# Scan masks merged ahead of one exponential, other PSUM banks for the first rows of the output projection, and another landing rule in the planner

## The chip, the cores and the metric

The kernel runs on one core of a Trainium2 chip. A core has five engines that work side by side, each through its own queue in order: TensorE (PE, with its weight loads PEld), VectorE (DVE), ScalarE (ACT), GpSimd (POOL) and SyncE (SP, which issues most transfers here). The metric is the device time of one execution in microseconds (us), lower being better; three executions of the kernel before took 971.27, 972.96 and 973.4 us, with the median 972.96.

## What is computed

One layer of a diffusion backbone over 512 latent tokens (width 1024) with a context of 256 tokens. Both are normalised, modulated and multiplied with one combined input matrix, and the result feeds two groups of heads: attention (16 heads; latent queries see latent and context keys) and a state-space scan that runs forwards and backwards (16 heads in 2 groups, chunks of 128 tokens). Both go through one output projection; a gated MLP with a width-3 convolution follows. The part that the change rewrites is the sum inside a chunk of the scan:

```python
def segment_decay(cum):
    diff = cum[..., :, None] - cum[..., None, :]
    mask = jnp.tril(jnp.ones((n, n), dtype=bool))
    return jnp.exp(jnp.where(mask, diff, -jnp.inf))
...
within = segment_decay(a_cum)
cb = jnp.einsum("bclgn,bcsgn->bcgls", cc, bc)
y_diag = jnp.einsum("bcgls,bcgels,bcsgep->bclgep", cb, within, xd)
...
y_x = ssd_output(st_xf[0], st_xf[1]) + flip(ssd_output(st_xb[0], st_xb[1]))
...
y = y + d_skip.reshape(SSD_GROUPS, HEADS_PER_GROUP, 1) * xs
```

For one head and one chunk the forward scan needs a matrix that is zero above the diagonal, the backward scan one that is zero below it. Both are multiplied by the same `cb` and by the same inputs, so that they can be added first.

## The kernel before, in words

All matrix products are split into a high and a low float32r part and summed as three products (lines 503, 757, 1184, 1314, 1546), so that a block of work is: DMA, a copy on ACT (L502), a subtraction on DVE or POOL (L503), and products of 128x512 or 128x256 on PE.

The program runs through these stages: the modulation and the gate of the scan (L689); the input projections with their convolutions (`xbc`, L757 to L803); the scan (`ssd`, once for each group of 8 heads) beside the attention (`pair_of_heads`, 8 pairs of heads, with `project` ahead of each); the output projection (`natural_gemm`, L1314); the MLP's up-projection (L757 again) and its down-projection (`sweep`, L1546).

**The masks.** In `ssd`, for two chunks at a time (`cp2`) and each of 8 heads (`e`), so 2 x 2 x 8 = 32 times in all, one step builds the mask of both directions for two chunks. PE spreads the running sums over the partitions with two products of 128x256 (L1031, `sel`) into one PSUM bank, then adds a table that holds 0 or -1e30 with one product of 128x512 (L1035, `capi` and `caps`). ACT takes four exponentials of 128x128 with a bias for each row (L1040: direction by chunk). POOL adds the two directions (L1044), and DVE multiplies the sum by `cbt`, the products of B and C (L1045). L1064 multiplies the result with the inputs. L1050 starts the chunk's output with the skip term, `xs` times `dsk`. The tables `capf` and `capb` come with the constants, and POOL copies them once (L772, L774).

**PSUM.** There are 8 banks of 512 columns. `bk.cut` hands them out by name. While the scan runs, all of its products share one bank, number 7 (`s`). Attention has banks 0 to 2 for scores (`sc`), 3 for its sums (`o`), 4 and 5 for transposes (`t`) and 6 for projections (`p`). When the scan is done, bank 7 joins `t`. The output projection then takes four pairs of banks for its four blocks of 128 rows, block 0 in banks 0 and 1, and so on to block 3 in banks 6 and 7.

**The order.** Nothing above is the order in which the engines run it. The program is first recorded, then `plan` sets the order of every engine's queue. It prices each instruction (`price`), runs a list schedule forwards and backwards (`Graph.schedule`), places the buffers (`Memory`), and repeats; the order it finds is imposed on the program. For a transfer it keeps the time at which the queue of transfers is free again, and expects the data when that transfer's own cost is over, with `DMA_WAIT` (910) and 0.8 of the cost (`DMA_ALONE`) on top, in `Graph.wait`.

## Time and profile before

| | |
|---|---|
| median of three executions | 972.96 us |
| the profiled execution's own time | 974.93 us |
| its span, first to last instruction | 973.1 us |
| what lies around the span | 1.83 us |
| PE, PEld, DVE, ACT, POOL busy, share of the span | 98%, 83%, 77%, 55%, 25% |
| the 32 mask steps begin and end | 193.0 and 402.0 us |
| granted TensorE clock, mean | 0.990 |

A busy PE is not a PE at its peak: products overlap in its pipeline, and a product's recorded time is longer than the distance to the next one. Idle time of an engine costs something only where another engine waits for it. In the lists of groups, a row gives the line, the engine, the operation, output<-input, the shape and the count, then the busy time in us, the mean of one in ns, and the idle time ahead of them with what ended it.

### The profile page before, as it was taken

What the parts mean: (1) busy time and instruction counts of PE and PEld (TensorE: products, weight loads), DVE (VectorE), ACT (ScalarE), POOL (GpSimd) and SP (SyncE); (2) the same over time, 40 slices, a digit from 0 to 9 for tenths busy, and PEclk for the clock granted to TensorE, in tenths of its full rate; (3) what the DMA queues carried; (4) which work ended last, traced back from release to release, by engine and by line L of the source; (5) the groups of instructions that cost most, each with busy time, mean ns of one, the idle gap of its engine ahead of it and who ended that gap; (6) DMA issues with size and microseconds to landing.
All of it is one profiled execution on the core that took longest, in us unless ns stands there. A gap on an engine that the chain in (4) does not pass through costs nothing.

```text
span 973.1 us, 14739 instructions
## 1 busy us (share of the span) xinstructions
PE 949.4 (98%) x5150; PEld 809.9 (83%) x5150; DVE 749.7 (77%) x1377; ACT 538.8 (55%) x1088; POOL 240.0 (25%) x249
## 2 busy tenths in 40 slices
PE   9999999999999999999999999999999999999995
PEld 8888898888788888888888887988888888887784
DVE  5898868888879887887899977945275332899898
ACT  4464337655777887789877215634223221447673
POOL 0001000846758455643000000000010150330021
PEclk7999999999999999999999999999999999999998
DMA  9933102011323432544668666233273212545783
GB/s 354 377 116 141 40 15 78 21 49 50 96 60 83 95 104 66 130 104 115 214 199 302 216 223 231 67 152 130 78 262 115 66 66 91 170 143 194 232 280 135
DMA packets 54586, 137.66 MB, mean 141 GB/s; under 512 B 8032, under 2 KB 10992, under 8 KB 54512
## 3 DMA queue, kind: packets, MB, share of 16 engines
q1 hardware_dynamic: 53712, 135.05, 42.9%
q10 hardware_dynamic: 800, 1.68, 0.5%
q8 instruction: 40, 0.66, 0.3%
q14 instruction: 34, 0.28, 0.1%
HBM read 114.63 MB, written 6.34 MB: 124 GB/s over the span
## 4 chain that ended last, share of the span: by engine, by line
PE 75%; DVE 14%; DMA 5%; ACT 3%; issue 3%; SPq 0%; POOL 0%; DVEq 0%; ACTq 0%; POOLq 0%
PE banks L757 40%; PE banks L1314 8%; DVE block L503 7%; PE banks L689 5%; PE banks L1184 4%; PE banks L1546 4%; DMA block<-block 2%; PE banks L1200 2%; DMA block<-in_wdn_dram 2%; PE banks L1212 2%; DVE smalls L1186 2%; DVE block L1539 1%; PE banks L1119 1%; PE banks L1016 1%; PE banks L601 1%
## 5 line engine op out<-in xcount | busy, mean ns | idle before, releaser
L757 PE MATMUL banks<-block,block 128*128 128x512 f32 (+1 forms) x2132 | 443.8, 361 | 2.4 <-DVE block L1410 2.0
L757 PEld LDWEIGHTS banks<-block,block 128*128 128x128 f32 x2132 | 357.2, 189 | 62.8 <-DVE block L1410 2.2
L503 DVE TENSOR_TENSOR block<-block,block 128x512 fp32r<-128x512 f32 (+4 forms) x316 | 248.5, 824 | 78.9 <-PE banks L757 34.3
L502 ACT ACTIVATE block<-block 128x512 fp32r<-128x512 f32 (+5 forms) x340 | 217.1, 665 | 139.9 <-PE banks L757 33.6
L1546 PE MATMUL banks<-block,block 128*128 128x512 f32 x462 | 108.7, 392 | 1.9 <-DVE block L503 1.6
L1546 PEld LDWEIGHTS banks<-block,block 128*128 128x128 f32 x462 | 86.0, 188 | 22.9 <-DVE block L503 4.5
L1184 PE MATMUL banks<-block,block 128*128 128x256 f32 (+1 forms) x384 | 97.2, 354 | 2.3 <-DMA block<-block 1.1
L503 DVE TENSOR_TENSOR block<-banks,block 128x256 fp32r<-128x256 f32 (+1 forms) x156 | 83.4, 556 | 12.4 <-ACT block L502 11.4
L1314 PE MATMUL banks<-block,block 128*128 128x512 f32 x384 | 89.2, 391 | 0.0
L1314 PEld LDWEIGHTS banks<-block,block 128*128 128x128 f32 x384 | 71.8, 188 | 14.5
L502 ACT ACTIVATE block<-banks 128x256 fp32r<-128x256 f32 (+1 forms) x156 | 74.1, 497 | 10.7 <-PE banks L1200 7.5
L1186 DVE TENSOR_REDUCE smalls<-banks 128x1 f32<-128x768 f32 x64 | 60.9, 952 | 18.3 <-PE banks L1184 12.7
L1188 ACT ACTIVATE block<-banks,smalls 128x768 f32<-128x768 f32 x64 | 57.9, 904 | 20.5 <-DVE smalls L1186 18.2
L1184 PEld LDWEIGHTS banks<-block,block 128*128 128x128 f32 x384 | 60.8, 189 | 9.7 <-ACT block L1188 2.6
L1200 PE MATMUL banks<-cst,block 128*128 128x128 f32 x384 | 66.4, 274 | 2.2 <-DVE block L503 2.1
L1212 PE MATMUL banks<-block,block 128*128 128x256 f32 x384 | 68.0, 294 | 0.2
L792 DVE SCALAR_TENSOR_TENSOR block<-banks,cwh,block 128x510 f32<-128x510 f32 (+3 forms) x88 | 51.5, 621 | 15.9 <-ACT block L788 15.1
L591 DVE SCALAR_TENSOR_TENSOR block<-block,block 128x1024 f32<-128x1024 f32 x52 | 62.4, 1216 | 0.5 <-PE banks L757 0.4
L1212 PEld LDWEIGHTS banks<-block,block 128*128 128x128 f32 x384 | 56.0, 190 | 4.4 <-DVE block L1245 0.5
L1441 ACT ACTIVATE block<-banks,prm 128x512 f32<-128x512 f32 x22 | 17.1, 777 | 73.2 <-PE banks L757 73.1
L1200 PEld LDWEIGHTS banks<-cst,block 128*128 128x128 f32 x384 | 47.5, 141 | 10.7 <-DVE block L503 4.2
L1040 ACT ACTIVATE block<-banks,block 128x128 f32<-128x128 f32 x128 | 42.1, 372 | 15.4 <-PE banks L1035 13.1
(230 smaller groups left out, 1104.3 us busy)
## 6 DMA issues: line engine op xcount, KB each, us to landing
block<-in_wdn_dram SPq DMA_DIRECT2D x99, 256.0 KB
block<-in_wmod_dram SPq DMA_DIRECT2D x48, 512.0 KB
block<-in_wup_dram SPq DMA_DIRECT2D x44, 512.0 KB
block<-block SPq DMA_DIRECT2D x32, 256.0 KB
block<-in_wout_dram SPq DMA_DIRECT2D x16, 512.0 KB
block<-in_wxbc_dram SPq DMA_DIRECT2D x12, 512.0 KB
block<-block SPq DMA_DIRECT2D x40, 128.0 KB
block<-in_wz_dram SPq DMA_DIRECT2D x16, 256.0 KB
```

The costliest lines, as they stand in the source:

```text
L502: act(hi, src, AF.Copy)
L503: (lo_eng or V).tensor_tensor(out=lo, in0=src, in1=hi, op=ALU.subtract)
L591: V.scalar_tensor_tensor(out=junk, in0=wt, scalar=0.5, in1=vec, op0=ALU.mult, op1=ALU.mult, accum_out=acc)
L757: mm(po, lhsT=wf(k, pt[0]), rhs=xf(k, pt[1]), start=(k == 0 and pt == parts[0]), stop=(k == nk - 1 and pt == parts[-1]))
L792: V.scalar_tensor_tensor(out=st[:, lo:hi], in0=pm[:, lo + d : hi + d], scalar=cwh[:, m * 5 + j : m * 5 + j + 1], in1=st[:, lo:hi], op0=ALU ...
L1184: mm(sc[:, o : o + n], lhsT=q_[:, x_, qi * P : (qi + 1) * P], rhs=kk[:, y_, :], start=part == 0, stop=part == 2)
L1186: V.reduce_max(nm, sc[:, :T], axis=AX.X, negate=True)
L1188: act(pe, sc[:, :T], AF.Exp, bias=nm, scale=1.0, accum_out=sum_)
L1200: nc.tensor.transpose((tx if c < NX else tc_)[:, o : o + P], pe[:, s_ : s_ + P], ident)
L1212: mm(po[:, half * 256 : half * 256 + 256], lhsT=vst(c), rhs=rhs, start=(part == 0 and c == 0), stop=(part == 1 and c == NKT - 1))
L1314: mm(po[i][:, nh * 512 : nh * 512 + 512], lhsT=l[lp][:, i * P : (i + 1) * P], rhs=w[wp][:, nh * 512 : nh * 512 + 512], start=(k == 0 and l ...
L1546: mm(po[i], lhsT=l[:, lp, i * P : (i + 1) * P], rhs=w[wp], start=first and q == 0 and n == 0, stop=q == PAIRS[-1] and n == 2, skip_group_c ...
```

## The change

Three edits are made together.

1. The masks. The product with the table and the tables themselves go. Of a mask, one triangle now comes from the forward direction and the other from the backward one, in one matrix. DVE adds to the forward half of the bank the difference of the two biases (`nbd`, two instructions of 128x128 that read PSUM), then copies the backward half over it wherever the table `trib` is not zero (`copy_predicated`, 128x256). ACT takes two exponentials of 128x128 instead of four, from SBUF instead of PSUM, and POOL multiplies by `cbt` straight away, so that DVE's product L1045 goes. On the diagonal both directions count, and only one is left there; what is missing, `dt` times the diagonal of `cbt`, moves into the skip term: for each group POOL cuts out the diagonal (one product of 128x512), DVE sums it (one `reduce_sum`) and makes `skip` with four small instructions.
2. The banks. The four pairs for the output projection are dealt in the reverse order, so that block 0 has banks 6 and 7, and bank 7 is taken out of `t` before the last pair of heads.
3. The planner. A transfer in a full queue is expected earlier: at the later of its own start plus 1.8 of its cost and the time the queue is free less `DMA_FULL` (600); `DMA_WAIT` stays. For a transfer that finds the queue empty the sum is as before. `price` gets a rule for `copy_predicated`.

```diff
-DMA_START, DMA_WAIT, DMA_AHEAD, DMA_ALONE, RUN, FLYING = 650, 910, 3000, 0.8, 80, 8
+DMA_START, DMA_WAIT, DMA_AHEAD, DMA_ALONE, RUN, FLYING, DMA_FULL = 650, 910, 3000, 0.8, 80, 8, 600
...
-        return DMA_WAIT + DMA_ALONE * self.cost[i] if self.dma[i] else WAITS.get((self.eng[i], self.eng[j]), 0)
+        return DMA_WAIT if self.dma[i] else WAITS.get((self.eng[i], self.eng[j]), 0)
...
-                end[i] = queue = max(t + self.dma[i] + DMA_START, queue) + self.cost[i]
+                began = t + self.dma[i] + DMA_START
+                queue = max(began, queue) + self.cost[i]
+                end[i] = max(began + (1 + DMA_ALONE) * self.cost[i], queue - DMA_FULL)
...
+    V.tensor_tensor(out=nbd, in0=nb[:, :NX, :16], in1=nb[:, :NX, 16:], op=ALU.subtract)
...
+        G.tensor_tensor(out=dg.rearrange("p (c n) -> p c n", c=NX), in0=cbt.rearrange("p (c n) -> p c n", c=NX),
+                        in1=ident.unsqueeze(1).to_broadcast([P, NX, P]), op=ALU.mult)
+        V.reduce_sum(cbd[:, g * NX : g * NX + NX], dg.rearrange("p (c n) -> p c n", c=NX), axis=AX.X)
+        for c in range(NX):
+            V.scalar_tensor_tensor(out=skip[:, c, g * 8 : g * 8 + 8], in0=dtb_[:, c, g * 8 : g * 8 + 8],
+                                   scalar=cbd[:, g * NX + c : g * NX + c + 1], in1=dsk[:, g * 8 : g * 8 + 8], op0=ALU.mult,
+                                   op1=ALU.add)
...
-                       rhs=chl[:, cp2 * 256 : cp2 * 256 + 256], start=dir_ == 0, stop=False)
-
-                mm(pdf, lhsT=capi, rhs=caps, start=False, stop=True)
-                df = t2()
-                for dir_ in range(2):
-                    for j in range(2):
-                        o = (dir_ * 2 + j) * P
-                        act(df[:, o : o + P], pdf[:, o : o + P], AF.Exp,
-                            bias=nb[:, cp2 * 2 + j, dir_ * 16 + h : dir_ * 16 + h + 1])
+                       rhs=chl[:, cp2 * 256 : cp2 * 256 + 256], start=True, stop=True)
+
+                df, at = t2(P, 2, P), slice(cp2 * 256, cp2 * 256 + 256)
+                for j in range(2):
+                    V.tensor_scalar(out=df[:, j, :], in0=pdf[:, j * P : (j + 1) * P], scalar1=nbd[:, cp2 * 2 + j, h : h + 1],
+                                    scalar2=None, op0=ALU.add)
+                V.copy_predicated(df, sooner, pdf[:, 256:].rearrange("p (c n) -> p c n", c=2))
                 pfree(pdf)
-                Me = M[e // 4][:, e % 4, :]
-                G.tensor_tensor(out=Me, in0=df[:, :256], in1=df[:, 256:], op=ALU.add)
-                V.tensor_tensor(out=Me, in0=Me, in1=cbt[:, cp2 * 256 : cp2 * 256 + 256], op=ALU.mult)
+                for j in range(2):
+                    act(df[:, j, :], df[:, j, :], AF.Exp, bias=nb[:, cp2 * 2 + j, 16 + h : 17 + h])
+                G.tensor_tensor(out=M[e // 4][:, e % 4, :], in0=df.rearrange("p c n -> p (c n)"), in1=cbt[:, at], op=ALU.mult)
...
+            if hp == NPAIR - 1:
+                bk.free["t"].remove(bank(7))
...
-    bk.cut(sc=[], o=[], t=[], p=[], a=[two(0), two(2), two(4), two(6)])
+    bk.cut(sc=[], o=[], t=[], p=[], a=[two(6), two(4), two(2), two(0)])
```

The planner's new prices move instructions nearly everywhere. Two places matter below. The first is DVE's queue in the third group of masks, where the second group of heads is scanned beside the attention. Before, in the kernel's own lines (L1186 is the softmax's maximum, L503 a low part, L1045 the mask's product):

```order
L503 TENSOR_TENSOR block_118_684<-banks,block_118_684 128x2x128
L503 TENSOR_TENSOR block_154_888<-banks,block_154_888 128x256
L1045 TENSOR_TENSOR block_498_3044<-block_498_3044,block_16_130 128x256
L1186 TENSOR_REDUCE smalls<-banks 128x1
L503 TENSOR_TENSOR block_374_2450<-banks,block_334_2263 128x4x128
L503 TENSOR_TENSOR block_118_684<-banks,block_118_684 128x2x128
L1045 TENSOR_TENSOR block_498_3044<-block_498_3044,block_16_130 128x256
L1186 TENSOR_REDUCE smalls<-banks 128x1
```

And after, where a line stands some lines lower or higher in the file (L1194 is the maximum, L504 a low part, L1047 the added bias, L1049 the copy under the table):

```order
L504 TENSOR_TENSOR block_343_2286<-banks,block_343_2286 128x2x128
L1047 TENSOR_SCALAR block_84_510<-banks,block_106_614 128x128 x2
L1194 TENSOR_REDUCE smalls<-banks 128x1
L1049 COPY_PREDICATED block_84_510<-block_74_468,banks 128x256
L504 TENSOR_TENSOR block_31_273<-banks,block_31_273 128x256
L504 TENSOR_TENSOR block_418_2644<-banks,block_116_681 128x4x128
L1047 TENSOR_SCALAR block_84_510<-banks,block_106_614 128x128 x2
L504 TENSOR_TENSOR block_118_683<-banks,block_118_683 128x2x128
L1049 COPY_PREDICATED block_84_510<-block_74_468,banks 128x256
```

Between two maxima stood one mask instruction, and it read SBUF alone; now three stand there, they read the scan's bank, and a maximum can lie between the first two and the third.

The second place is PE's queue where attention ends and the output projection begins. Before (L1212 is attention's last product, L1314 the output projection):

```order
L1212 MATMUL banks<-block_718_4483,block_160_948 128x256 x4
L1314 MATMUL banks<-block_284_1940,block_719_4484 128x512
L1314 MATMUL banks<-block_441_2799,block_719_4484 128x512
L1212 MATMUL banks<-block_486_2966,block_94_524 128x256 x2
L1212 MATMUL banks<-block_676_4200,block_160_948 128x256 x4
L1314 MATMUL banks<-block_284_1940,block_719_4484 128x512
L1212 MATMUL banks<-block_486_2966,block_94_524 128x256 x2
L1314 MATMUL banks<-block_284_1940,block_719_4484 128x512
```

And after (L1220 is attention's last product, L1324 the output projection, L1208 a transpose of the softmax):

```order
L1220 MATMUL banks<-block_657_4033,block_757_4687 128x256 x2
L1324 MATMUL banks<-block_797_5045,block_25_230 128x512 x2
L1208 MATMUL banks<-cst,block_788_4941 128x128 x2
L1324 MATMUL banks<-block_161_944,block_25_230 128x512
L1220 MATMUL banks<-block_632_3787,block_159_939 128x256 x4
L1324 MATMUL banks<-block_161_944,block_25_230 128x512
L1324 MATMUL banks<-block_797_5045,block_25_230 128x512
L1324 MATMUL banks<-block_161_944,block_25_230 128x512
L1220 MATMUL banks<-block_685_4220,block_757_4687 128x256 x2
```

Ahead of attention's last product, 21 products of the output projection stand in the queue before, and 24 after. In the output projection's own run PE's order is the same as before for some 400 products.

More of the change, by code (lines that the diff above doesn't have):

```diff
@@ L33 @@
 GRID_W = 64
-BIG = 1e30
 PRM = {}
@@ L65, in constants @@
     put("trib", (i[:, None] >= i[None, :]))
-    put("capf", np.where(i[:, None] <= i[None, :], 0.0, -BIG))
-    put("capb", np.where(i[:, None] >= i[None, :], 0.0, -BIG))
     rot = np.zeros((64, P))
```

30 lines of the change are left out of this document (16 added, 14 removed).

## The prediction

> **What bounds the kernel now.** I read the page first: the span, each engine's busy time, and the chain that ended last.
>
> ```profile
> span 973.1 us, 14739 instructions
> PE 949.4 (98%) x5150; PEld 809.9 (83%) x5150; DVE 749.7 (77%) x1377; ACT 538.8 (55%) x1088; POOL 240.0 (25%) x249
> PE 75%; DVE 14%; DMA 5%; ACT 3%; issue 3%; SPq 0%; POOL 0%; DVEq 0%; ACTq 0%; POOLq 0%
> ```
>
> PE is busy for 98% of the span, and three quarters of the chain are PE's own work. The last quarter is what PE waited for, above all DVE (14%). These shares serve below as weights: a microsecond taken from PE is worth at least 0.75 us, one put on DVE costs 0.14 us on average, one taken from ACT brings 0.03 us.
>
> Then the stages, by windows. The first row is the stretch from the first mask step to the last, the second what follows up to the output projection, the third a stretch of the up-projection in which PE waits for nothing, the fourth the fullest stretch of DVE that I found among the masks.
>
> ```profile
> 193.00:402.00 209.00, 206.20 (x1268) 178.13 (x1267) 176.86 (x298) 156.14 (x390) 124.76 (x121) 1.00 0.30 76
> 402.00:514.00 112.00, 108.75 (x751) 97.15 (x751) 93.16 (x167) 91.38 (x196) 31.71 (x37) 1.00 0.57 162
> 802.00:826.00 24.00, 24.00 (x108) 19.88 (x106) 6.56 (x11) 3.27 (x7) 0.69 (x1) 1.00 0.28 88
> 292.00:316.00 24.00, 23.59 (x143) 19.94 (x142) 23.11 (x33) 18.45 (x41) 21.05 (x20) 1.00 0.32 83
> ```
>
> The columns are the length, then busy time of PE, PEld, DVE, ACT and POOL, the granted clock, and the DMA share. While the masks are made PE is busy for 206.2 of 209 us, DVE for 176.9 (85%), ACT for 156.1 (75%). So PE leads there, and DVE is the next engine, with 32 us to spare.
>
> **The change part by part.** The masks' rows, and the nearest rows for what is new:
>
> ```profile
> L1031 PE MATMUL banks<-block,sel 128*128 128x256 f32 x64 | 14.2, 291 | 0.4 <-DVE block L1066 0.3
> L1035 PE MATMUL banks<-block,capi 128*128 128x512 f32 x32 | 12.7, 396 | 0.0
> L1314 PE MATMUL banks<-block,block 128*128 128x512 f32 x384 | 89.2, 391 | 0.0
> L1040 ACT ACTIVATE block<-banks,block 128x128 f32<-128x128 f32 x128 | 42.1, 372 | 15.4 <-PE banks L1035 13.1 <-POOL block L1044 1.3 <-DVE block L503 0.7
> L1044 POOL TENSOR_TENSOR block<-block 128x256 f32<-128x256 f32 x32 | 29.8, 935 | 36.9 <-ACT block L1040 28.7 <-issue 5.4 <-PE banks L757 2.8
> L1045 DVE TENSOR_TENSOR block<-block,block 128x256 f32<-128x256 f32 x32 | 20.2, 652 | 2.1 <-POOL block L1044 2.0
> L503 DVE TENSOR_TENSOR block<-banks,block 128x256 fp32r<-128x256 f32 x74 | 30.3, 415 | 4.3 <-ACT block L502 3.8
> L503 DVE TENSOR_TENSOR block<-banks,block 128x512 fp32r<-128x512 f32 x82 | 55.5, 683 | 8.1 <-ACT block L502 7.6 <-PE banks L1200 0.2
> L1410 DVE SCALAR_TENSOR_TENSOR block<-banks,mod,block 128x128 fp32r<-128x128 f32 x32 | 10.0, 340 | 0.5 <-ACT block L1409 0.4
> L533 DVE SCALAR_TENSOR_TENSOR smalls<-smalls 128x1 f32<-128x1 f32 x48 | 7.4, 157 | 0.6
> ```
>
> *PE loses L1035.* One product lasts 396 ns in the record, but overlaps its neighbours. In a full queue one of 128x512 takes 24.00 us / 108 = 0.222 us by the window and 89.2 / 384 = 0.232 us by L1314. So 32 products are worth 7.1 to 7.4 us of queue; I take 7.3. The two products of L1031 stay. If PE were the chain throughout the masks, all 7.3 us would come off; by the weight of 0.75 it is 5.5. I take 5.5 and keep 7.3 for the range.
>
> *DVE gains.* L1045 goes, 20.2 us. For each of 32 steps come two added biases of 128x128 from PSUM. The nearest row is L1410, the same size from PSUM, with a second tensor: 0.340 us. Half of L503's 0.415 us for 256 columns, 0.208, is the lower bound. I take 0.27. The copy under the table reads 256 columns of PSUM and a table in SBUF, as L503 reads PSUM and SBUF: 0.415 us at least. It shows nowhere before; if it passed its two sources in turn it would be as long as L503 with 512 columns, 0.683. I take 0.45, near the row of its own size. The sum is 64 x 0.27 + 32 x 0.45 = 31.7 us (26.6 to 43.6). For each group a sum over 512 columns (as L503, 0.68) and four small instructions (as L533, 0.16) add 2 x 1.3 = 2.6 us. The net is 31.7 + 2.6 - 20.2 = +14 us, between +9 and +26. The 32 us that DVE has to spare beside PE hide most of it; by the weight of 0.14 it costs 2.0 us (1.3 to 3.6).
>
> The Trainium skill, "SBUF — State Buffer", says that a GpSimd instruction and a VectorE instruction with two SBUF inputs lock each other out of a shared pair of ports for a whole instruction. The trace agrees: L1045, with two SBUF inputs, means 652 ns, L503 of the same size with one input in PSUM 415. By that rule the new instructions, which read PSUM, are never held, DVE's net falls to the lower bound of +9 us, and its cost to 1.3.
>
> *ACT loses half its exponentials.* 128 of them take 42.1 us, 0.33 each. 64 stay, reading SBUF and no longer PSUM; from SBUF they are not shorter, and at most as long as the recorded 0.372. So ACT gives back 42.1 - 64 x 0.36 = 19 us, worth 0.03 x 19 = 0.6 us. POOL has 32 instructions of the same size in L1044's place, and three or four more at the start of the groups; it is no part of the chain (0%), and its 209 - 124.8 = 84 us of idle time among the masks hide them.
>
> *The scan's bank.* One step of the third group, in order of time:
>
> ```profile
> 323.33 0.50 PE L1031 MATMUL banks<-block,sel 128*128 128x256 f32 x2
> 323.67 0.40 PE L1035 MATMUL banks<-block,capi 128*128 128x512 f32 x1
> 324.16 1.14 ACT L1040 ACTIVATE block<-banks,block 128x128 f32<-128x128 f32 x4 [0.46 <-PE banks L1035]
> 325.43 0.74 POOL L1044 TENSOR_TENSOR block<-block 128x256 f32<-128x256 f32 x1 [3.16 <-ACT block L1040]
> ```
>
> Bank 7 is held from 323.33 until the exponentials end at 325.30, 2.0 us. After, PE needs 0.2 us less, and three DVE instructions (2 x 0.27 + 0.45 = 1.0 us) take the place of 1.14 us of ACT; where a maximum stands between them, as in the order above, the bank is held a maximum longer. I cost this at nothing, since PE has attention's products meanwhile; without that cover it is one maximum for a part of the 32 steps, and that is the first rival's matter.
>
> *The banks of the output projection.* PE's rows at the handover:
>
> ```profile
> 514.15 0.94 PE L1314 MATMUL banks<-block,block 128*128 128x512 f32 x3
> 515.29 1.86 PE L1314 MATMUL banks<-block,block 128*128 128x512 f32 x7
> 517.61 0.99 PE L1200 MATMUL banks<-cst,block 128*128 128x128 f32 x6 [0.45 <-DVE block L503]
> 522.40 0.86 PE L1314 MATMUL banks<-block,block 128*128 128x512 f32 x3
> ```
>
> The output projection already fills gaps here, since block 3 had bank 6 early. The new order brings 24 instead of 21 products ahead of attention's end: 3 x 0.23 = 0.7 us at most, if each fills a hole. Against it the last pair has two banks for transposes and no longer three, and PE's waits at transposes are the longest of its list:
>
> ```profile
> PE banks L1200 <- DVE block L503: 2.1, 5, 0.6
> PE banks L757 <- DVE block L1410: 2.0, 1, 2.0
> PE banks L1546 <- DVE block L503: 1.6, 3, 1.1
> ```
>
> Five waits make 2.1 us there; doubling them costs 2.1. So this part lies between -0.7 and +2.1 us; I take -0.2, near the first, since the order shows other products beside the transposes.
>
> *The planner.* Its landing rule matters only where the queue of transfers is full: the first 50 us, the output projection, the down-projection. In the first, SP's order is the same at the start; in the second, PE's is the same for 400 products. What can change is in waits like the last row, 1.6 us. The rest is that every queue in the middle is dealt anew. I take 0, with +-2 us.
>
> The sum: -5.5 + 2.0 - 0.6 - 0.2 + 0 = -4.3 us. The profiled execution took 974.93 us (span 973.1 and 1.83 around it), 1.97 above the median of 972.96; from it the sum gives 970.6, from the median 968.7. I forecast 968.5.
>
> **The rivals.** *DVE takes over from PE among the masks, and the kernel is slower.* It would have 176.9 + 14 = 190.9 us to do in a stretch that PE would leave in 209 - 7.3 = 201.7: 95% full. The fourth window shows that DVE can be so full (23.11 of 24), but only for 24 us. If it reaches 90% in the mean, the stretch takes 190.9 / 0.90 = 212 us, 3 longer than now; at the upper bound of +26 it takes 225, 16 longer. From 0.90 x 209 - 176.9 = 11.2 us of added work on, this decides. For it speaks that the new instructions stand between PE's product and the bank's release, among the softmax's maxima; against it that the planner can spread the masks over the 112 us behind (DVE 83%), and that ACT is eased. The price is +3 to +16; I put it at +4, 977 us. The Trainium skill, "Perfetto Trace Analysis", section "Optimizing Scalar/DVE Operations", says that work may move from DVE to Scalar where DVE is saturated, and that each DVE instruction on PSUM pays about 125 ns beside its elements. The change goes the other way, with 96 such instructions, 12 us by the page (an estimate); no run yet shows whether 85% counts as saturated.
>
> *Nothing comes of it.* PE's products gone, the chain runs through the softmax (score, maximum, exponential, transpose), which waits for DVE as before, and new waits of 7 us take the place of the work. Then the time is 973, within 2 us. For it speaks the quarter of the chain that is not PE's; against it the 98.7% of PE among the masks.
>
> *More than the sum.* If all 7.3 us come off, ACT's 13.1 us of waits for L1035 go with its in-order queue, and half of PE's listed 5.7 us of waits above close, the gain is 7.3 + 2.9 = 10 us: 963.
>
> **How the numbers follow.** This kernel's runs can tell about 0.2%, 2 us, from no change. I give the forecast (2 to 8 us faster) 0.52, more than that 0.18, nothing 0.15, DVE in the lead 0.15. Faster is then 0.70, same 0.15, slower 0.15. The range from 961 to 974.5 holds the forecast, nearly all of the case of no change, and the larger gain up to 12 us (its 10, and the planner's 2 on top); it leaves out most of the slower case and the end of the larger gain, some 0.2. The bounds of the unknown prices (-7.3 + 1.3 - 0.6 - 0.7 - 2 = -9.3; -5.5 + 3.6 - 0.6 + 2.1 + 2 = +1.6) give 963.7 to 974.6 and lie in it but for 0.1 us.
>
> **What would show it.** After the change the row of L1035 is gone and PE's busy time is about 7 us less; the exponentials are 64 with 21 to 24 us; the added biases come at 0.21 to 0.34 us and the copy at 0.42 to 0.68; DVE's busy time grows by 9 to 26 us, and PE's share of the stretch of masks stays at 98% or more. The sum is wrong if the stretch from the first mask to the output projection is not 4 to 8 us shorter, if PE's waits for DVE there grow by more than 3 us, or if the gain lies outside of it, at the handover or in the stages with a full queue.

## The result, and the profile after

The changed kernel takes 977.88 us (median of 20 runs, 972.12 to 983.47); the kernel before, beside it on the same chip, 972.83. The ratio is 1.0057 with a 95% interval from 1.0041 to 1.0072: the change makes the kernel 0.6% slower, 5.5 us. The prediction was 968.5, within 961 to 974.5.

The profiled execution of the kernel after is one of its quicker ones (976.18 us, span 974.4). First its page: the span, the busy time of each engine, the chain that ended last.

```profile
span 974.4 us, 14684 instructions
PE 946.4 (97%) x5118; PEld 805.6 (83%) x5118; DVE 768.6 (79%) x1452; ACT 525.2 (54%) x1024; POOL 244.3 (25%) x246
PE 75%; DVE 14%; DMA 4%; ACT 3%; issue 2%; SPq 0%; POOL 0%; DVEq 0%; ACTq 0%
```

PE has 32 instructions less and DVE is busy for 18.9 us more (768.6 against 749.7), yet the shares of the chain are those of before. They say nothing of what happened.

Next the groups of the mask step. L1041 are the two products that stayed, L1047 the added biases, L1049 the copy under the table, L1052 the exponentials, L1053 the product on POOL.

```profile
L1041 PE MATMUL banks<-block,sel 128*128 128x256 f32 x64 | 14.2, 298 | 3.0 <-DVE block L1049 2.4 <-DVE block L1031 0.6
L1047 DVE TENSOR_SCALAR block<-banks,block 128x128 f32<-128x128 f32 x64 | 21.1, 342 | 1.1 <-PE banks L1041 0.8
L1049 DVE COPY_PREDICATED block<-block,banks 128x256 f32<-128x256 int32 x32 | 14.2, 443 | 0.3
L1052 ACT ACTIVATE block<-block,block 128x128 f32<-128x128 f32 x64 | 22.6, 397 | 7.5 <-DVE block L1049 5.8 <-DVE smalls L533 1.6
L1053 POOL TENSOR_TENSOR block<-block,block 128x256 f32<-128x256 f32 x32 | 24.4, 767 | 35.4 <-ACT block L1052 25.8 <-PE banks L1192 4.0 <-DVE block L504 2.8
```

The products of L1041 waited 0.4 us in all before (L1031 then); now it is 3.0 us, 2.4 of it for L1049, the copy that ends the use of the bank.

Then two windows. Of the kernel before, the first 16 mask steps and all 64 products of the masks:

```profile
193.00:260.70 67.70, 67.39 (x399) 57.91 (x398) 57.34 (x95) 42.99 (x110) 41.68 (x36) 1.00 0.20 52
193.00:396.50 203.50, 200.70 (x1231) 173.02 (x1230) 171.75 (x289) 151.29 (x379) 122.20 (x117) 1.00 0.29 74
```

and of the kernel after, the same two stretches:

```profile
217.60:267.60 50.00, 46.60 (x283) 40.33 (x282) 46.98 (x105) 33.07 (x77) 34.35 (x34) 1.00 0.37 97
217.60:394.60 177.00, 168.02 (x1048) 144.95 (x1047) 158.91 (x324) 129.37 (x298) 110.75 (x112) 1.00 0.32 83
```

The planner begins the masks 24 us later and packs them closer. PE's share falls from 98.6% (200.70 / 203.50) to 94.9%, and in the first sixteen steps to 93%, where DVE stands at 94% (46.98 / 50.00). PE, which led before, stands for 9.0 us of the 177 (177.00 - 168.02), where it stood for 2.8 of 203.5. The longest of these waits in the kernel after (us in total, times, longest; L1192 are attention's scores, L1196 its exponential, L503 a copy on ACT, L1127 a product of `project`, L1031 the scan's sum):

```profile
PE banks L1041 <- DVE block L1049: 2.4, 2, 1.9
PE banks L1192 <- DMA block<-block: 2.0, 2, 1.2
PE banks L1192 <- ACT block L1196: 1.6, 3, 1.0
PE banks L1127 <- ACT block L503: 1.6, 1, 1.6
PE banks L1041 <- DVE block L1031: 0.6, 1, 0.6
```

and in the kernel before (L1200 is a transpose of the softmax, L1056 a product of the scan):

```profile
PE banks L1200 <- DVE block L503: 0.8, 2, 0.4
PE banks L1056 <- DVE block L1058: 0.4, 1, 0.4
```

With the smaller rows, 3.5 us of them end with DVE (1.5 before), 3.4 with ACT (0.8 before) and 2.0 with a transfer (none before). So this trace puts 2 us of the 6 added on DVE directly; whether DVE also stands behind the others is not shown in it.

One of these waits, in order of time (columns: start, length, engine, instruction, idle time before it and what ended it; rows between are left out):

```profile
260.26 0.51 PE L1041 MATMUL banks<-block,sel 128*128 128x256 f32 x2
...
260.69 0.48 DVE L788 SCALAR_TENSOR_TENSOR block<-banks,cwh,block 128x254 f32<-128x254 f32 x1
261.09 0.34 DVE L1047 TENSOR_SCALAR block<-banks,block 128x128 f32<-128x128 f32 x1
...
261.35 0.47 DVE L788 SCALAR_TENSOR_TENSOR block<-banks,cwh,block 128x255 f32<-128x255 f32 x1
...
261.74 0.34 DVE L1047 TENSOR_SCALAR block<-banks,block 128x128 f32<-128x128 f32 x1
262.00 0.48 DVE L788 SCALAR_TENSOR_TENSOR block<-banks,cwh,block 128x255 f32<-128x255 f32 x1
...
262.39 0.43 DVE L1049 COPY_PREDICATED block<-block,banks 128x256 f32<-128x256 int32 x1
...
262.88 0.38 PE L1041 MATMUL banks<-block,sel 128*128 128x256 f32 x1 [1.89 <-DVE block L1049]
```

Between the added biases and the copy stand instructions of the convolution (L788), DVE never rests, and the bank that PE began to fill at 260.26 comes free at 262.82, 2.6 us later; in the step that the prediction shows it was 2.0. PE stands for 1.89 us. Three DVE instructions lie between PE's product and the bank's release, and each of them queues behind whatever DVE has to do.

### The profile page after: what moved, and what is told of

It reads as the page before. It is cut to its first block, busy times and chain, and to the rows that moved or that the text cites. A ratio compares the mean times of both kernels' runs of the same rounds, so it can differ in the third digit from the quotient of the medians.

```text
span 974.4 us, 14684 instructions
## 1 busy us (share of the span) xinstructions
PE 946.4 (97%) x5118; PEld 805.6 (83%) x5118; DVE 768.6 (79%) x1452; ACT 525.2 (54%) x1024; POOL 244.3 (25%) x246
## 4 chain that ended last, share of the span: by engine, by line
PE 75%; DVE 14%; DMA 4%; ACT 3%; issue 2%; SPq 0%; POOL 0%; DVEq 0%; ACTq 0%
PE banks L758 38%; PE banks L1324 6%; DVE block L504 6%; PE banks L1192 5%; PE banks L1556 5%; PE banks L690 5%; PE banks L1220 3%; PE banks L1208 3%; DVE block L1549 2%; DMA block<-in_wdn_dram 2%; PE banks L1127 1%; ACT block L503 1%; PE banks L1026 1%; PE banks L602 1%; DMA block<-block 1%
## 5 line engine op out<-in xcount | busy, mean ns | idle before, releaser
L758 PE MATMUL banks<-block,block 128*128 128x512 f32 (+1 forms) x2132 | 452.0, 362 | 2.4 <-DVE block L1420 1.6
L503 ACT ACTIVATE block<-block 128x512 fp32r<-128x512 f32 (+4 forms) x340 | 215.6, 663 | 173.8 <-PE banks L758 42.3
L504 DVE TENSOR_TENSOR block<-block,block 128x512 fp32r<-128x512 f32 (+3 forms) x316 | 249.3, 825 | 53.3 <-PE banks L758 36.2
L1556 PE MATMUL banks<-block,block 128*128 128x512 f32 x462 | 109.1, 392 | 1.3 <-DVE block L504 1.0
L504 DVE TENSOR_TENSOR block<-banks,block 128x512 fp32r<-128x512 f32 (+1 forms) x156 | 84.2, 556 | 16.7 <-ACT block L503 16.0
L1192 PE MATMUL banks<-block,block 128*128 128x512 f32 (+1 forms) x384 | 92.8, 350 | 4.3 <-ACT block L1196 2.2
L1324 PE MATMUL banks<-block,block 128*128 128x512 f32 x384 | 89.4, 391 | 0.0
L503 ACT ACTIVATE block<-banks 128x512 fp32r<-128x512 f32 (+1 forms) x156 | 74.0, 495 | 26.2 <-PE banks L1208 9.6
L1324 PEld LDWEIGHTS banks<-block,block 128*128 128x128 f32 x384 | 71.7, 188 | 14.5
L1220 PE MATMUL banks<-block,block 128*128 128x256 f32 x384 | 69.1, 295 | 2.6 <-ACT block L503 2.3
L1192 PEld LDWEIGHTS banks<-block,block 128*128 128x128 f32 x384 | 59.7, 189 | 11.5 <-ACT block L1196 3.4
L592 DVE SCALAR_TENSOR_TENSOR block<-block,block 128x1024 f32<-128x1024 f32 x52 | 65.7, 1280 | 3.8 <-DMA block<-in_wmod_dram 2.1
L1194 DVE TENSOR_REDUCE smalls<-banks 128x1 f32<-128x768 f32 x64 | 60.8, 950 | 6.9 <-PE banks L1192 5.4
L1196 ACT ACTIVATE block<-banks,smalls 128x768 f32<-128x768 f32 x64 | 57.6, 900 | 15.6 <-DVE smalls L1194 14.7
L1208 PE MATMUL banks<-cst,block 128*128 128x128 f32 x384 | 65.5, 273 | 0.0
L1220 PEld LDWEIGHTS banks<-block,block 128*128 128x128 f32 x384 | 56.1, 189 | 6.5 <-ACT block L503 2.6
L788 DVE SCALAR_TENSOR_TENSOR block<-banks,cwh,block 128x510 f32<-128x510 f32 (+3 forms) x88 | 51.7, 621 | 12.2 <-ACT block L784 11.4
L1208 PEld LDWEIGHTS banks<-cst,block 128*128 128x128 f32 x384 | 47.1, 141 | 7.6 <-DVE block L504 1.1
L1465 POOL TENSOR_TENSOR block<-block 128x256 f32<-128x256 f32 x11 | 10.9, 999 | 167.5 <-ACT block L1456 74.7
L690 PE MATMUL banks<-block,block 128*128 128x512 f32 x192 | 49.9, 407 | 0.0
```

Source lines behind the costliest of these rows:

```text
L503: act(hi, src, AF.Copy)
L504: (lo_eng or V).tensor_tensor(out=lo, in0=src, in1=hi, op=ALU.subtract)
L592: V.scalar_tensor_tensor(out=junk, in0=wt, scalar=0.5, in1=vec, op0=ALU.mult, op1=ALU.mult, accum_out=acc)
L690: mm(po[i], lhsT=hx[k][:, hp, i * P : (i + 1) * P], rhs=wz[wp], start=(k == 0 and wp == 0 and hp == 0), stop=(k == KD - 1 and hp == 1))
L758: mm(po, lhsT=wf(k, pt[0]), rhs=xf(k, pt[1]), start=(k == 0 and pt == parts[0]), stop=(k == nk - 1 and pt == parts[-1]))
L1192: mm(sc[:, o : o + n], lhsT=q_[:, x_, qi * P : (qi + 1) * P], rhs=kk[:, y_, :], start=part == 0, stop=part == 2)
```

## The experiments

Three theories are tried. The prediction's: PE leads among the masks, DVE's added time is mostly hidden, the planner only deals. Its first rival's: among the masks DVE's time is itself the price. A third: the planner's rule costs something. (The expectations give letters to theories of their own, each where it stands.) Each ratio below is to the kernel before on the same chip, which stood at 971.3 to 972.8 us, and the difference is what the ratio has above or below 1, times 972 us. The ratio can lie 0.2% from that of the two medians (e5_masks_planner: 977.98 / 972.63 = 1.0055).

| kernel | median us | ratio, 95% interval | difference |
|---|---|---|---|
| after | 977.88 | 1.0057 [1.0041, 1.0072] | +5.5 |
| e1_masks | 967.38 | 0.9957 [0.9937, 0.9976] | -4.2 |
| e2_planner | 977.15 | 1.0049 [1.0031, 1.0068] | +4.8 |
| e3_banks | 971.34 | 0.9994 [0.9977, 1.0010] | -0.6 |
| e4_planner_banks | 972.38 | 0.9995 [0.9969, 1.0021] | -0.5 |
| e5_masks_planner | 977.98 | 1.0076 [1.0052, 1.0100] | +7.4 |
| e6_masks_banks | 974.46 | 1.0024 [1.0003, 1.0044] | +2.3 |
| e7_after_2nd | 976.81 | 1.0057 [1.0035, 1.0078] | +5.5 |
| e8_masks_2nd | 971.47 | 0.9996 [0.9980, 1.0012] | -0.4 |
| e9_drop | 966.49 | 0.9940 [0.9918, 0.9961] | -5.8 |
| e10_dve | 981.29 | 1.0093 [1.0061, 1.0126] | +9.0 |
| e11_graft | 977.81 | 1.0061 [1.0041, 1.0080] | +5.9 |
| e12_before_2nd | 968.39 | 0.9962 [0.9940, 0.9983] | -3.7 |
| e13_dve_off | 976.91 | 1.0053 [1.0034, 1.0073] | +5.2 |
| e14_onebias | 974.11 | 1.0020 [0.9997, 1.0044] | +1.9 |
| e15_actbias | 965.64 | 0.9920 [0.9895, 0.9944] | -7.8 |
| e16_planner_2nd | 975.60 | 1.0041 [1.0023, 1.0059] | +4.0 |
| e17_start_order | 972.83 | 1.0013 [0.9991, 1.0034] | +1.3 |
| e18_actbias_after | 966.56 | 0.9943 [0.9916, 0.9970] | -5.5 |

**The parts by themselves.** The diff was cut into its three parts.

*e1_masks*: the masks and the price of the copy, without the other two parts.

```diff
-                    mm(pdf, lhsT=capi, rhs=caps, start=False, stop=True)
+                    V.tensor_scalar(out=df[:, j, :], in0=pdf[...], scalar1=nbd[...], op0=ALU.add)
+                V.copy_predicated(df, sooner, pdf[:, 256:]...)
```

> The new masks alone, with the planner and the banks of before. The changed kernel took 977.9 us against 972.8. Theory A (VectorE leads among the masks): the loss comes from the masks, this kernel is 975 to 979 us, and the stretch from the first mask's stage to attention's end is longer than before by 2 us or more although the 32 products of 7.3 us are gone. Theory B (the planner's rule spoils the start): the masks alone bring what was forecast, 965 to 970 us, and the first product of the gate's stage comes at the same time as before, 21 us. Theory C (the banks): as B, 965 to 970.

*e2_planner*: the rule alone.

```diff
-                end[i] = queue = max(t + self.dma[i] + DMA_START, queue) + self.cost[i]
+                end[i] = max(began + (1 + DMA_ALONE) * self.cost[i], queue - DMA_FULL)
```

> The planner's landing rule alone. Its queue of TensorE in the first 25 us is word for word that of the changed kernel. Theory B: 975 to 979 us, TensorE's clock stays at half for 17 us at the start as in the changed kernel's trace and not for 13.7, the first product of the gate's stage comes 2 us later, and the rest of the kernel is as long as before. Theory A: within 2 us of before, 971 to 975. Theory C: within 2 us of before.

*e3_banks*: the banks alone.

```diff
-    bk.cut(sc=[], o=[], t=[], p=[], a=[two(0), two(2), two(4), two(6)])
+    bk.cut(sc=[], o=[], t=[], p=[], a=[two(6), two(4), two(2), two(0)])
```

> The banks of the output projection alone. Theory C (one bank less for the last pair's transposes): 975 to 977 us, with a wait of TensorE for a high or low part of a transpose near the end of attention that is over 1 us longer than before. Theories A and B: within 2 us of before, 971 to 975.

*e4_planner_banks*: the edits of e2_planner and e3_banks together.

> All but the masks: the planner's rule and the banks, with the masks of before. Theory A: within 2 us of before, 971 to 975, so that the masks make the rest of the way to 977.9. Theory B: 975 to 979, as the planner's rule alone; then the masks, put on top, would have changed the time by less than 3 us. Theory C: as the banks alone, 975 to 977.

The masks alone gain 4.2 us, as the sum had it; for the banks nothing is shown (-2.2 to +1.0); the rule alone costs 4.8, and with the banks nothing. The clock at the start, which the expectation of e2_planner blames, is not the reason: in the trace of e2_planner it stood at half for 10 us of the first 24, as in that of the kernel before, and in the kernel after's for over 13; yet e2_planner is nearly as slow as the kernel after, and the mean clock over its runs is no lower than before's beside it (0.993 against 0.988). The parts do not add: -4.2 + 4.8 - 0.6 = 0, and the whole costs 5.5.

**Pairs, and second-best orders.** Each edit makes the planner deal the whole program anew, so a single number holds the edit and its deal.

*e5_masks_planner* and *e6_masks_banks*: the edits of e1_masks with those of e2_planner, and with those of e3_banks.

> The new masks and the planner's rule, the banks left as before (beside the kernel before at 972.7). Theory A, the loss belongs to the pair of masks and rule (the rule makes the planner crowd the new mask steps): 976 to 979 us, like the changed kernel, and the first state product starts more than 10 us later than before. Theory B, every edit deals the whole order anew and the deal is worth several us either way: anywhere between 964 and 978, with no relation to the changed kernel's 977.9.

> The new masks and the banks, the planner's rule left as before. Theory A, the loss needs the rule: 965 to 969 us, like the masks alone at 967.4. Theory B, a matter of the deal: anywhere between 964 and 978; 971 or more would speak for it.

*e7_after_2nd*, *e8_masks_2nd*, and later *e12_before_2nd* and *e16_planner_2nd*: the same instructions, in the order that the planner rated second of its 24 tries, in effect:

```diff
-    return found
+    return sorted(tries, key=lambda f: f[0])[1]
```

> The changed kernel with every instruction the same, in the order that its planner rated second of its 24 (959.0 us by its own count, 0.5 more than the one it took). Theory A, a loss of the edits themselves: 976 to 980 us. Theory B, a matter of the deal: more than 3 us away from 977.9, with 50 per cent chance below 973.

> The new masks alone, in the order that the planner rated second (961.7 us by its own count, 1.1 more than the one it took, which ran in 967.4). Theory A: 966 to 970 us. Theory B: more than 3 us away from 967.4, so 970.5 or more, or 964.3 or less.

> The kernel before, every instruction the same, in the order that its planner rated second of 24 (966.8 us by its own count, 1.9 more than the one it took). If the order that was taken is no better on the chip than its neighbours: 970 to 976 us. If the kernel before is itself a lucky deal: 976 to 980, and the new masks would then have to be held against 976 and not against 972.7.

> The planner's rule alone (nothing else changed), in the order that it rated second (966.6 us by its own count). The five kernels dealt under the new rule stood at 977.1, 972.4, 978.0, 977.9 and 976.8, the six under the old one at 972.7, 971.3, 967.4, 974.5, 971.5 and 968.4. If the rule costs of itself: 974 or more. If it only drew badly: as the orders of the kernel before, 968 to 972.5.

The kernel before in its second order is 3.7 us faster than in its first, which the planner rated 1.9 us better; the masks in their second order lose nearly all of the 4.2 us they gained. So a deal alone moves this kernel by up to 4 us, and e1_masks had drawn well. Averages say more: under the old rule the six kernels stand at 0, -0.6, -3.7 with the old masks (mean -1.4) and -4.2, +2.3, -0.4 with the new (mean -0.8); under the new rule at +4.8, -0.5, +4.0 (mean +2.8) and +7.4, +5.5, +5.5 (mean +6.1). In neither row do the new masks gain, though with three kernels each their difference is uncertain by 2.2 us (one standard error) and a gain of 4 is not ruled out. The new rule's mean stands 5.5 us above the old one's, with a standard error of 1.5.

The granted clock adds to the scatter: over the executions of one kernel a mean clock lower by 0.01 goes with a time longer by some 5 us (an estimate from all runs of the experiments, with the clock of each). The mean clock of each of these kernels lies within 0.005 of that of before beside it; taking this out moves single kernels by up to 2 us, and leaves the rule's mean at 5.4.

**Prices at a fixed order.** These kernels hold the order and the buffers of the kernel before (of the changed kernel in e14_onebias) as a table of numbers, so that no deal is in them.

*e9_drop*: the cap products out (the masks are not cut at the diagonal).

```diff
-                mm(pdf, lhsT=capi, rhs=caps, start=False, stop=True)
...
-                        act(df[:, o : o + P], pdf[:, o : o + P], AF.Exp, bias=nb[...])
+                        act(df[:, o : o + P], pdf[:, o : o + P], AF.Exp, scale=0.02, bias=E[...])
```

> The kernel before with its own order and buffers held, instruction for instruction, and only the 32 cap products left out (the masks are then not cut at the diagonal; the exponentials get a scale and a bias that keep them finite, at the same size). It prices the first term of the sum alone: 5.5 us off by the prediction, so 967 (7.3 at most, 965.4). Rival, that other work of the softmax sets the pace there: less than 3 us off, 970 or more.

The busy times on its page:

```profile
PE 943.4 (98%) x5118; PEld 804.9 (83%) x5118; DVE 748.1 (77%) x1377; ACT 538.6 (56%) x1088; POOL 241.4 (25%) x249
```

5.8 us off, from 3.8 to 8.0, with PE busy for 6.0 us less (943.4 against 949.4) and DVE nearly as before: the first term of the sum is right.

*e10_dve*: one more DVE instruction behind the exponentials of each step.

```diff
+                V.tensor_tensor(out=pdf[:, :256], in0=pdf[:, :256], in1=cbt[:, :256], op=ALU.mult)
                 pfree(pdf)
```

> The kernel before with its order and buffers held, and one more DVE instruction in each mask step, behind the four exponentials: 128x256 from the step's bank, times the cbt tile, back into the bank (its result is not used). By the row of L503, 0.415 us each, 13.3 us of DVE in all, near the 18.9 that the change adds, and the bank held half a us longer. By the prediction's weight of 0.14 it costs 1.9 us, 974.6. Theory that DVE has become the limit among the masks: 5 us or more, 977.7 or later, and the stretch of the masks longer by as much.

Its group, and the one of the products that need the bank next:

```profile
L1042 DVE TENSOR_TENSOR banks<-banks,block 128x256 f32<-128x256 f32 x32 | 13.7, 429 | 10.7 <-ACT block L1040 10.2
L1031 PE MATMUL banks<-block,sel 128*128 128x256 f32 x64 | 15.8, 315 | 4.7 <-DVE banks L1042 3.8 <-DVE block L1067 0.3 <-DVE block L1021 0.2
```

13.7 us of work and 10.7 us in which DVE stood at the head of its queue, waiting for ACT: 24.4 us of DVE gone, 9.0 us of time, 0.37 for each. The weight of 0.14 gave 1.9. But a bank was held longer too, so this run alone does not tell DVE's time from the bank.

*e11_graft*: the new mask steps in the old order (without the diagonal's second term).

```diff
-                mm(pdf, lhsT=capi, rhs=caps, start=False, stop=True)
...
+                    V.tensor_scalar(out=df[:, j, :], in0=pdf[...], scalar1=nbd[...], op0=ALU.add)
+                V.copy_predicated(df, sooner, pdf[:, 256:]...)
```

> The new mask steps set into the order and the buffers of the kernel before, everything else where it stood: no cap product, on DVE two added biases and the copy under the table where the first exponential stood, two exponentials where the third and fourth stood, one product on POOL, none on DVE. It leaves out the diagonal's second term (8 small instructions, 2 sums and 2 products per kernel). No deal of the planner is in it. If the prediction's sum holds at a fixed order: 967 to 970 us. If DVE in the lead gives the product's time back: 971.5 to 977.

The group of its exponentials, with the idle time before them:

```profile
L1043 ACT ACTIVATE block<-block,block 128x128 f32<-128x128 f32 x64 | 23.9, 396 | 30.4 <-DVE block L1040 26.4 <-DVE block L1216 1.9 <-POOL block L1132 1.7
```

5.9 us slower, beyond both times that were expected, and 11.7 above e9_drop: what the product gave is given back twice over. Here ACT also stands 26.4 us before its exponentials, waiting for DVE's copy (L1040 in this kernel); the planner's own order avoids most of that (5.8 us in the kernel after), so this is no clean price of DVE's time.

*e13_dve_off*: DVE loaded with a reciprocal that holds no bank and that nobody waits for.

```diff
+                V.reciprocal(idle, idle)
                 pfree(pdf)
```

> The kernel before with its order and buffers held, and in each mask step one more DVE instruction that nobody waits for and that holds no bank: a reciprocal in place over 56 columns of a tile of its own. By the rows of RECIPROCAL (193 ns for 8 columns, 1345 for 192) it takes 0.49 us, 15.8 us in all, where the instruction in e10_dve took 13.7 us and waited 10.7 at the head of DVE's queue. If DVE's own time is what costs: 5 to 10 us slower than before, as e10_dve (0.4 or more us for each). If it was the bank held longer and DVE blocked behind a wait: by the prediction's weight 2 us, no more than 3.

The group of the added instruction, which waits for nothing:

```profile
L1043 DVE RECIPROCAL idle<-idle 128x56 f32<-128x56 f32 x32 | 15.8, 494 | 0.1
```

and the window from its first to its last product of the masks:

```profile
190.40:395.40 205.00, 201.21 (x1229) 172.46 (x1229) 181.52 (x319) 151.81 (x379) 121.36 (x117) 1.00 0.29 74
```

15.8 us of DVE cost 5.2 us (3.3 to 7.1), 0.33 for each, with no bank held and nobody waiting for the result. Records of neighbours overlap, so DVE's busy time in all grows by 10.4 us only (760.1 against 749.7); by that measure it is 0.50 for each. DVE is busy for 181.5 of the 205 us of the masks, 89%, where it was 84%. The price rests on the medians: the profiled execution is the fastest of the twelve (973.37 us), its masks take 1.5 us longer than before's 203.5, and it doesn't show where the rest lies.

*e14_onebias*: the changed kernel in its own order, one added bias in place of two.

```diff
-                for j in range(2):
-                    V.tensor_scalar(out=df[:, j, :], in0=pdf[:, j * P : (j + 1) * P], scalar1=nbd[...], ...)
+                V.tensor_scalar(out=df..., in0=pdf[:, :256], scalar1=nbd[...], ...)
...
-                    act(df[:, j, :], df[:, j, :], AF.Exp, bias=nb[...])
+                    act(df[:, j, :], df[:, j, :], AF.Exp, scale=0.02, bias=E[...])
```

> The changed kernel with its order and buffers held, and one added bias over 256 columns in each mask step in place of two over 128 (it leaves out the second chunk's own bias, and a scale in the exponentials keeps them finite). DVE has 7 to 8 us less: 32 x 0.42 in place of 21.1 us. If DVE's time among the masks is the price: 3 us or more faster than the changed kernel, 974.5 or less where that stands at 977.5. By the weight of 0.14: 1 us faster, 976.5.

The group of the one bias:

```profile
L1046 DVE TENSOR_SCALAR block<-banks,block 128x256 f32<-128x256 f32 x32 | 15.3, 477 | 1.2 <-PE banks L1041 1.1
```

DVE has 5.8 us less (15.3 against 21.1), and the kernel is 3.6 us faster than the changed one (+1.9 against +5.5): 0.62 for each, though the two intervals leave 1 to 6 us. That DVE's time is dearer in the changed kernel than in the one before would fit, but is not shown.

*e15_actbias*: the new masks, old rule, old banks, the added biases on ACT.

```diff
-                    V.tensor_scalar(out=df[:, j, :], in0=pdf[:, j * P : (j + 1) * P], scalar1=nbd[...], scalar2=None, op0=ALU.add)
+                    act(df[:, j, :], pdf[:, j * P : (j + 1) * P], AF.Identity, bias=nbd[...])
```

> The new masks alone (the planner's rule and the banks as before) with the added biases given to ACT: two ACT instructions with a bias from the bank in place of the two on DVE; the copy under the table stays on DVE. PE loses its 7.3 us, DVE has 20.2 - 14.2 - 2.6 = 3.4 us less than the kernel before, ACT about 5 us more. If DVE's added time was what ate the products' gain, this version keeps it: 963 to 968 us (5 to 6 below before, and a deal of the planner of +-3). If it was something else in the new step, such as the longer chain of engines: 969 to 975, like the new masks' other deals (967.4, 971.5, 974.5).

The groups of the biases on ACT and of the copy:

```profile
L1044 ACT ACTIVATE block<-banks,block 128x128 f32<-128x128 f32 x64 | 22.8, 375 | 3.5 <-PE banks L1038 3.2
L1045 DVE COPY_PREDICATED block<-block,banks 128x256 f32<-128x256 int32 x32 | 14.1, 445 | 12.0 <-ACT block L1044 10.2 <-DMA block<-sums 1.4 <-issue 0.3
```

and the window from its first to its last product of the masks:

```profile
210.60:387.40 176.80, 171.54 (x1071) 148.28 (x1070) 148.32 (x265) 142.55 (x360) 110.71 (x111) 1.00 0.32 83
```

7.8 us faster than before, 12 to 13 faster than the changed kernel, and the best time of all. The stretch of the masks is as long as in the kernel after (176.8 against 177.0 us), but PE does 171.5 us in it instead of 168.0, and DVE is at 84% instead of 90%. ACT, at 81%, carries the biases for less: 375 ns each, and 3.5 us of waiting for PE. But DVE's share by itself does not set the pace. The same window of e1_masks, under the same rule and with the biases on DVE:

```profile
205.50:390.50 185.00, 179.63 (x1114) 155.67 (x1113) 171.20 (x331) 133.53 (x306) 115.08 (x114) 0.99 0.29 74
```

There DVE is at 93%, fuller than in the kernel after, and PE still at 97%, as here. How much PE waits at a given share of DVE differs from order to order.

*e17_start_order*: TensorE's first 76 rows and DVE's first 64 as the new rule orders them, in the kernel before. L621 are the sums over a loaded block, which the rule expects sooner, L682 products that only fill. Of PE's rows, in order (the trace has two records for each row of L621):

```diff
-L666 x2, L621 x4, L666 x4, L621 x4, L666 x2, L682 x3, L621 x4, L682 x1, L621 x4, L682 x12
+L621 x4, L666 x2, L621 x4, L666 x5, L621 x4, L666 x1, L682 x2, L621 x4, L682 x14
```

> The kernel before with its order and buffers held, except that TensorE's first 76 rows and DVE's first 64 stand as the planner's new rule orders them (the same instructions; sums over a loaded block stand ahead of filling products). If the rule's cost lies in the start: 1 to 3 us slower than before, 973 to 975, and the first z product some 1.5 us later. If the start costs nothing and the rule's cost lies in the middle: within 0.8 us of before.

1.3 us, from -0.9 to +3.3: the start alone does not account for the rule's 5 us, and whether it costs anything isn't settled. In the traces the first product of the gate's stage (L689) comes at 22.89 us, before at 21.16.

*e18_actbias_after*: the whole change with the biases on ACT, the edit of e15_actbias in the kernel after.

> The whole change (masks, banks, the planner's new rule) with the added biases given to ACT in place of DVE. If DVE's time and the rule are two separate costs that add: the rule's 5 us stay on top of the 965.6 of the new masks with the biases on ACT, so 969 to 972.5, 6 to 9 below the changed kernel. If the rule costs only where DVE is full: 964 to 968. If easing DVE does not help here: 975 or more.

5.5 us faster than before, 11 faster than the changed kernel. The edit of 64 instructions that moves these biases off DVE makes the new masks 5.5 to 7.8 us faster than the kernel before under either rule, and the rule costs 2.3 us here, less than the two intervals can tell from nothing. Each of the two is one deal, and a deal alone moves up to 4 us; the 11 us here are beyond that.

## Why the prediction was wrong

*PE loses L1035: -5.5 us.* Right: -5.8 (e9_drop). PE's busy time fell by 6.0 us there; in the kernel after it fell by 3.0 only, where 7 had been named as the sign.

*DVE gains, "by the weight of 0.14 it costs 2.0 us".* **This is the step that failed.** The instructions' count was right and their size near: the copy takes 443 ns (0.45 taken), the added bias 342 (0.27 taken, 0.34 the upper bound), so the net is +18.9 us instead of +14, inside the +9 to +26. The price of each us was wrong. It measures 0.33 where DVE was loaded in the kernel before (e13_dve_off) and, with a wide interval, 0.62 where it was relieved in the one after (e14_onebias). As an estimate that makes 18.9 x 0.33 to 18.9 x 0.62, 6 to 12 us, and not 2; the low end of e13_dve_off's interval, 3.3 us for 15.8, still makes 4. By DVE's busy time in all, in which the 18.9 are counted, the two prices are 0.50 and 0.68 (3.6 us for 768.6 - 763.3), and it is 9 to 13. The 0.14 was DVE's share of the chain over the whole span. That share tells where the end was decided in one execution; it is not the price of adding work. In the stretch that got the work DVE was at 84% already (171.75 / 203.5) and went to 90%, in parts to 94%, with its instructions queued in order between PE's product and the release of PE's bank. "The 32 us that DVE has to spare beside PE hide most of it" treated a mean of 85% as room; e13_dve_off, which only fills that room, costs a third of what it fills.

*ACT: -19 us, worth 0.6.* Its size was right (42.1 to 22.6, an exponential from SBUF at 397 ns and not the 360 taken). That time was idle afterwards, and e15_actbias shows its use: 22.8 us of it hold the biases.

*The scan's bank, "I cost this at nothing".* Wrong: L1041 waits 3.0 us against 0.4, 2.4 of it in two waits for the copy that frees the bank, and the step above holds its bank 2.6 us instead of 2.0. The cover, attention's products, wasn't always there.

*The banks of the output projection: -0.2.* Not contradicted: -0.6, from -2.2 to +1.0.

*The planner: 0, +-2 us.* Too narrow. A deal by itself moves this kernel by up to 4 us (e12_before_2nd, e8_masks_2nd), which was to be had from no view. And six orders under the new rule stand 5.5 us (+-1.5) above six under the old. What in the rule costs this is open: the start alone is not shown to cost it (e17_start_order), with DVE eased it falls to 2.3 (e18_actbias_after) and between the two kernels with the banks but the old masks it is 0.1 (e4_planner_banks against e3_banks). That it costs most where DVE is fullest was not shown apart from the deals.

So of the miss of 10 us (-4.3 forecast, +5.5 measured), by these estimates, taken at their low end, about half is DVE's price, which turns the masks' gain into nothing (-0.8 against -1.4 in the means, uncertain by 2.2), and about half the new rule's orders. The first rival, given 0.15, had the place and that DVE's time is paid for. That its time (977) came out is in part luck: it knew nothing of the rule's half, its stretch of 212 us did not come (177, begun later and packed closer), and its limit of 90% of DVE is matched in the kernel after (158.91 / 177) but passed in e1_masks (93%), which was faster. Of the prediction's signs against itself one came, PE below 98% among the masks (94.9%); another, PE's waits for DVE from the first mask to the output projection longer by over 3 us, did not: they went from 2.6 to 3.9 us. A third, the length of that stretch, can't be read, since the masks begin 24 us later.

Of the two rules of the Trainium skill that the prediction weighed, the lock between GpSimd and a VectorE instruction with two SBUF inputs ("SBUF — State Buffer", section "SBUF: two separate sides") led to the lower bound for the new DVE instructions, +9. The trace has them at 342 and 443 ns, +18.9: that neither reads two tensors from SBUF did not make them cheap. The Trainium skill, "Perfetto Trace Analysis", section "Optimizing Scalar/DVE Operations", says that handing work to Scalar may make sense where DVE is saturated. By that rule the change moved its work the wrong way, and the runs agree: with the same 64 biases on DVE the kernel was slower than with them on ACT by 3.6 and 7.4 us under the old rule (e1_masks and e8_masks_2nd against e15_actbias) and by 11.0 under the new one (the kernel after against e18_actbias_after), the deals included.

## What to carry to other kernels

Do not price work added to an engine by its share of the chain over the span; look at the stretch that gets it, and measure the price at a fixed order. Here DVE was busy for 84% of that stretch, with 32 us to spare, and each added us cost about a third of a us and not a seventh. When an edit goes through a planner, one timing holds the edit and a deal; time a second-best order of each side, or hold the order fixed, before believing a difference of half a per cent. And look for the engine that the edit eases: with the biases on ACT, the new masks were the fastest version.

## What the runs showed of the hardware

- A DVE instruction with a bias for each partition, read from PSUM, took 342 ns for 128 columns and 477 for 256 (the rows of L1047 and of e14_onebias): by these two points (an estimate) 207 ns that do not depend on the width, and 1.05 ns for each column. A record overlaps the next one here (an L1047 starts at 261.09, the L788 before it ends at 261.17), so 64 of 128 columns kept DVE busy for 21.1 us, and 32 of 256 for 15.3.
- A copy under a table of int32, from PSUM, took 443 ns for 256 columns, hardly more than a product of the same size from PSUM and back (429 in e10_dve).
- A DVE reciprocal took 494 ns for 56 columns, beside 193 for 8 and 1345 for 192: 6.3 ns for each column.
- An exponential of 128x128 took 396 to 413 ns from SBUF (e11_graft, e15_actbias) and 372 from PSUM; an added bias on ACT from PSUM 375.
- A mean granted clock lower by 0.01 went with a time longer by some 5 us, among executions of the same kernel. In the first 24 us the clock stood at half for 10 us in the trace of the kernel before, for over 13 in that of the kernel after, and never in that of e17_start_order.
